# Token-major blocks turned by DMA instead of TensorE, and the two halves of the down product summed as one group

## The chip, the cores and the metric

The kernel runs on one core of a Trainium2 chip. The metric is the time of one execution on the device in microseconds (us). The engines are PE (TensorE; PEld is its weight load), DVE (VectorE), ACT (ScalarE), POOL (GpSimd) and SP (SyncE, whose queue issues nearly all DMAs here).

## The reference

A decoder trunk of two layers on 512 tokens of width 1024. Each layer is a feed-forward half step, a mixing step of three kinds of attention, and a second feed-forward half step:

```
def _swiglu(t, w_gate, w_up, w_down):
    return (jax.nn.silu(t @ w_gate) * (t @ w_up)) @ w_down

mem_n = _rmsnorm(mem, mem_norm_g)
for l in range(DEPTH):                      # 2
    f = _swiglu(_rmsnorm(h, ffn1_pre_g[l]), ffn1_w_gate[l], ffn1_w_up[l], ffn1_w_down[l])
    h = h + 0.5 * _rmsnorm(f, ffn1_post_g[l])
    ...                                     # mixing; uses mem_n @ w_mem_kv[l]
    f = _swiglu(_rmsnorm(h, ffn2_pre_g[l]), ffn2_w_gate[l], ffn2_w_up[l], ffn2_w_down[l])
    h = h + 0.5 * _rmsnorm(f, ffn2_post_g[l])
```

D_FF is 2816, which is 22 tiles of 128. Everything is float32.

## The kernel before

A float32 product is made of three matmuls (`mm3`, lines 204 to 206): each operand is split into a high and a low part, h = copy on ACT (L181), l = x - h on DVE (L182).

There are four feed-forward blocks, named a0, c0, a1, c1. In each, 16 of the 22 hidden tiles are computed in two halves (ci = 0, 1) of eight tiles, by a block scheme with seven products in place of eight: `token_products` makes the gate products G and the up products U, `products` the down products d. Tokens and columns are cut in two, a product multiplies sums of blocks, and `ORDER`, `SUM` and `TO` say in which order the seven run, into which pair of PSUM banks each adds up, and which block of the result is finished by it. One product is 24 matmuls of 128x512. The other six hidden tiles (16 to 21) are plain products: `halved`, `gates` and `ups`, called g and u in the plan, and their part of the down product is `down`, which also adds everything up and starts the normalisation of the next step.

G and U come out token-major: a block has tokens on the partitions. The down products need the hidden axis on the partitions. So after U's products n = 1, 4, 5 and 6 the finished block (gate times up, 128 x 1024 words, two token tiles by four hidden tiles) is turned by `turn` (L790): eight TensorE transposes into two PSUM banks (L800) and two copies to SBUF on ACT (L802). They are traced in the middle of the next product. `hidden_rows` holds the turned blocks.

`product` (L844) runs a down product. `first_factor` (L824) builds its left operand one product ahead. For the first half the results are copied to the f tiles (L874, L877) and added (L875, L879); the second half runs the same seven products again into other banks and adds its results to f on DVE; its n = 1 starts from a copy of f back into PSUM (L855).

The order of the work is a queue `Q` of jobs. A job has weight units and a generator of PE work. Before a job runs, its units are loaded, and the units of the jobs behind it, four units ahead (`load_ahead`): a load is a DMA on SP (`fetch`), for most block units a subtraction (L326), and the split. Buffers come from rings by tag: "wh" and "wl" have four buffers, a product uses two of each; raw weights use two "raw" and, within a block, two to four "o" buffers; first factors use "v" (six); the scratch tag of `tmp` has five; PSUM has four banks "z" and four "mm". `PLAN` is the list of jobs of a feed-forward block. In it a plain product (one of two tiles of a pair) follows every two down products:

```
PLAN = 7 * [("G", 0)] + [("m", 0)] + 7 * [("U", 0)] + 7 * [("G", 1)] + 6 * [("U", 1)] + [("a", 0), ("U", 1)]
downs = iter(6 * [("d", 0)] + [("a", 1), ("d", 0)] + 7 * [("d", 1)])
```

Instructions are put in order on each engine at build time by a scheduler that works with modelled durations; `keep_in_program_order` pins an instruction behind the one traced before it on the same engine. Each engine then runs its list strictly in order.

In the a blocks the memory input is normalised as well: `mem_norm` loads two tiles, scales them (L1034), transposes them on TensorE (L1041) and writes the split result (L1046, L1047). It is a job of its own (`aside`) ahead of `down`; its users are the memory keys (pmk) and values.

Of the kernel before, what the change touches and what calls it, by code (L numbers as in the profile page):

```python
# [9 lines left out]
F32 = mybir.dt.float32  # L10
F32R = mybir.dt.float32r
BF16 = mybir.dt.bfloat16
AF = mybir.ActivationFunctionType
# [9 lines left out]
def kernel(  # L23
# [578 lines left out]
    def ffn(l, src, wg, wu, wd, dst, name, spare, parked, plan, aside=None):  # L602
# [7 lines left out]
        hr = {}  # L610
# [128 lines left out]
        def token_product(ci, up, n, uns):  # L739
# [13 lines left out]
            for un in uns:  # L753
                for k in range(un.nk):
# [6 lines left out]
                    if kk == ND // 2 - 2:  # L761
                        yield from turn("z")
# [24 lines left out]
            if up and n in (1, 4, 5, 6):  # L787
                st["turn"] = (f"{nm}", g, r)

        def turn(tag):  # L790

            nm, g, r = st.pop("turn", (None, None, None))
            if nm is None:
                return
            g = g.rearrange("p f q -> p (f q)")
            for b in range(2):
                pt = pbank(tag, f"ht{nm}_{b}")
                for f in range(2):
                    for e in range(2):
                        nc.tensor.transpose(pt[:, (2 * f + e) * P:(2 * f + e + 1) * P],  # L800
                                            g[:, e * S + (2 * b + f) * P:][:, :P], ident[:])
                nc.scalar.copy(r[:, 2 * b:2 * b + 2], pt[:].rearrange("p (f q) -> p f q", f=2))  # L802
                yield 0.4
# [40 lines left out]
        def product(ci, n, uns):  # L844
            if n == 0 and ci == 0:
                RINGS["o"] = 2
                dst.begin()
            if n < 6:
                first_factor(ci, n + 1)
            if n in (0, 1, 2):  # L850
                st["b", SUM[n]] = [pbank("z", f"pd{name}_{ci}_{n}_{e}") for e in range(2)]
            pts = st["b", SUM[n]]
            if n == 1 and ci:
                for e in range(2):
                    nc.scalar.copy(pts[e][:], dst.fs[e][:, HF[0]])  # L855
            h, l = st["a", ci, n]
            opens, ends = n in (0, 2) or (n == 1 and not ci), n in (1, 4, 6)
            for un in uns:
                for k in range(un.nk):
# [6 lines left out]
                    if kk == FC // 2 - 2:  # L866
                        yield from turn("mm")
            if n == 0:
                return
            i, hf = TO[n]  # L870
            for e in range(2):
                f = dst.fs[2 * i + e][:, HF[hf]]
                if n == 1:
                    nc.scalar.copy(f, st["b", 0][e][:])  # L874
                    nc.vector.tensor_tensor(f, f, pts[e][:], ALU.add)  # L875
                elif ci == 0 and n in (2, 3, 6):
                    nc.scalar.copy(f, pts[e][:])  # L877
                else:
                    nc.vector.tensor_tensor(f, f, pts[e][:], ALU.add)  # L879

        def products(ci):

            keep = Keep(lambda k0: stile([P, 2, S], "o", f"bt{name}_{ci}_{k0}", F32)[:])
            w = wd[l, ci * FC * P:(ci + 1) * FC * P]
            for n in range(7):
                uns = [BlockUnit(n, w, FC // 2, k, 2, S, keep, f"d{name}_{ci}_{n}_{k}", ("raw", "o")[k // 2])
                       for k in range(0, FC // 2, 2)]
                if n == 4:
                    for un, of in zip(uns, had):
                        un.inherits(of)  # L890
                had = uns
                yield uns, (lambda n=n, uns=uns: product(ci, n, uns))
# [18 lines left out]
        def queue(what):  # L911
# [13 lines left out]
            else:  # L925
                if what not in made:
                    made[what] = products(n) if kind == "d" else token_products(n, kind == "U")
# [11 lines left out]
        if aside is not None:  # L939
            Q.add([], aside)  # L940
        hact = lambda k, c=FULL: (hid[f0 + k][:, 0, c], hid[f0 + k][:, 1, c])
        down(wd[l, f0 * P:], NF - f0, hact, f"d{name}", dst, marks, back, down_from)
        return marks

    def down(w, ktiles, act, name, dst, marks, before, begun=None):
# [52 lines left out]
        Q.add(uns[0], first)  # L998
        marks["next"] = [], []
# [697 lines left out]
```

## Time and profile before

| what | value |
|---|---|
| median of 3 runs | 2390.12 us (2388.59 to 2391.15) |
| profiled execution | 2389.31 us |
| its span, first to last instruction | 2387.6 us |
| mean granted TensorE clock | 0.998 |
| DMA | 338.23 MB, q1 busy 44.3% of 16 engines' span |

The page gives the busy time of each engine, its share of the span and the number of its instructions. A table by stretch gives, for each stretch from:to in us, its length, then for each engine the busy time and in brackets the count of instructions, then the granted clock, the share of the DMA engines and GB/s. A row of a timeline has start, duration, engine, line, operation, written tile <- read tiles, shape and count. A group row has line, engine, operation, tiles, shapes and count, then busy us and mean ns, then the engine's idle time before them with what ended it. In rows by line the three numbers behind a count are the shortest, median and longest duration in ns. A wait row has the waiting engine, tile and line, whom it waited for, us in total, times, and the longest.

### The profile page before, as it was taken

Reading aid. Unit: us, or ns where it says so; the run is one execution under the profiler, and the core shown is the slowest. Engines: PE = TensorE matmul, PEld = TensorE weight load, DVE = VectorE, ACT = ScalarE, POOL = GpSimd, SP = SyncE. Lnnn points to the kernel's source line nnn. Section 1 sums busy time; section 2 is a strip of 40 time slices with the busy share of each in tenths; the row PEclk is TensorE's granted clock in tenths of the full one; section 3 lists DMA queues with packets and bytes.
Section 4 is the critical chain, followed back from the end, with each engine's and each line's share of the span. In section 5 each row is a group of like instructions: output and inputs, shape, how many; then the busy total and the mean of one; then the engine's idle time right before and its main releaser. Section 6 shows DMA issues by size and latency. Waiting matters only on the chain.

```text
span 2387.6 us, 31555 instructions
## 1 busy us (share of the span) xinstructions
PE 2370.0 (99%) x11975; PEld 2006.6 (84%) x11975; DVE 1844.2 (77%) x2414; ACT 1425.1 (60%) x2250; POOL 75.1 (3%) x134
## 2 busy tenths in 40 slices
PE   9999999999999999999999999999999999999998
PEld 7888889888888888888888888888888888888887
DVE  8878877577777688788788788766777767887885
ACT  6655555576766555555655554656777664655554
POOL 1000000000111000000000000000001100000000
PEclk9999999999999999999999999999999999999999
DMA  6554455223323655444645554542323235555444
GB/s 205 184 150 158 142 189 147 80 82 87 89 72 106 195 175 175 144 158 157 206 140 167 150 176 156 187 116 71 98 71 97 80 115 198 164 176 154 154 140 153
DMA packets 232173, 338.23 MB, mean 142 GB/s; under 512 B 10683, under 2 KB 125395, under 8 KB 232021
## 3 DMA queue, kind: packets, MB, share of 16 engines
q1 hardware_dynamic: 231924, 336.18, 44.3%
q8 instruction: 94, 1.54, 0.3%
q14 instruction: 59, 0.48, 0.1%
q0 software_dynamic: 96, 0.03, 0.0%
HBM read 319.39 MB, written 16.78 MB: 141 GB/s over the span
## 4 chain that ended last, share of the span: by engine, by line
PE 89%; DVE 5%; DMA 3%; ACT 2%; issue 1%; SPq 0%; POOL 0%; DVEq 0%; ACTq 0%
PE pg L205 3%; PE pg L204 3%; PE pg L206 3%; PE pda L205 3%; PE pda L206 3%; PE pda L204 3%; PE pdc L205 3%; PE pdc L206 2%; PE pdc L204 2%; PE pb L206 1%; PE pb L205 1%; PE pb L204 1%; PE pq L205 1%; PE pq L204 1%; PE pq L206 1%
## 5 line engine op out<-in xcount | busy, mean ns | idle before, releaser
L204 PE MATMUL pg<-us_a,wh_wg 128*128 128x512 f32 x384 | 150.9, 393 | 0.0
L205 PE MATMUL pg<-us_a,wh_wg 128*128 128x512 f32 x384 | 149.8, 390 | 0.0
L206 PE MATMUL pg<-us_a,wl_wg 128*128 128x512 f32 x384 | 149.7, 390 | 0.0
L205 PE MATMUL pda<-wl_da,aha 128*128 128x512 f32 x224 | 87.6, 391 | 0.6 <-DVE wl_da L182 0.5
L205 PE MATMUL pdc<-wl_dc,ahc 128*128 128x512 f32 x224 | 87.5, 391 | 0.3 <-DVE wl_dc L182 0.3
L204 PE MATMUL pda<-wh_da,aha 128*128 128x512 f32 x224 | 87.4, 390 | 0.0
L204 PE MATMUL pdc<-wh_dc,ahc 128*128 128x512 f32 x224 | 87.4, 390 | 0.0
L206 PE MATMUL pda<-wh_da,ala 128*128 128x512 f32 x224 | 87.2, 389 | 0.0
L206 PE MATMUL pdc<-wh_dc,alc 128*128 128x512 f32 x224 | 87.2, 389 | 0.0
L206 PEld LDWEIGHTS pg<-us_a,wl_wg 128*128 128x128 f32 x384 | 72.1, 188 | 15.2
L204 PEld LDWEIGHTS pg<-us_a,wh_wg 128*128 128x128 f32 x384 | 72.1, 188 | 14.1
L205 PEld LDWEIGHTS pg<-us_a,wh_wg 128*128 128x128 f32 x384 | 72.2, 188 | 14.1
L182 DVE TENSOR_TENSOR wl_dc<-raw_dc,wh_dc 128x1024 fp32r<-128x1024 f32 x50 | 61.1, 1223 | 29.3 <-ACT wh_dc L181 29.1
L181 ACT CAST wh_dc<-raw_dc 128x1024 fp32r<-128x1024 f32 x50 | 52.6, 1053 | 43.9 <-PE pdc L206 15.1
L182 DVE TENSOR_TENSOR wl_da<-raw_da,wh_da 128x1024 fp32r<-128x1024 f32 x50 | 61.1, 1223 | 22.3 <-ACT wh_da L181 22.0
L181 ACT CAST wh_da<-raw_da 128x1024 fp32r<-128x1024 f32 x50 | 52.7, 1055 | 39.3 <-PE pda L206 15.0
L185 DVE SCALAR_TENSOR_TENSOR wl_wg<-raw_wg,wh_wg 128x1024 fp32r<-128x1024 f32 x48 | 58.4, 1220 | 21.6 <-ACT wh_wg L184 21.6
L199 DVE SCALAR_TENSOR_TENSOR ga<-pg,bgate,ga 128x512 f32<-128x512 f32 x48 | 35.9, 747 | 49.5 <-ACT ga L198 49.5
L181 ACT CAST wh_uc<-raw_uc 128x1024 fp32r<-128x1024 f32 x44 | 46.3, 1053 | 43.5 <-PE pwc1u L206 10.3
L181 ACT CAST wh_ua<-raw_ua 128x1024 fp32r<-128x1024 f32 x44 | 46.2, 1053 | 34.3 <-PE pwa1u L206 10.3
L184 ACT ACTIVATE wh_wg<-raw_wg 128x1024 fp32r<-128x1024 f32 x48 | 50.5, 1057 | 24.0 <-PE pv L1088 11.7
L182 DVE TENSOR_TENSOR wl_uc<-raw_uc,wh_uc 128x1024 fp32r<-128x1024 f32 x44 | 53.7, 1220 | 14.3 <-ACT wh_uc L181 14.2
(655 smaller groups left out, 8044.4 us busy)
## 6 DMA issues: line engine op xcount, KB each, us to landing
raw_da<-in_ffn_w_down_dram SPq DMA_DIRECT2D x66, 512.0 KB, 4.6
raw_dc<-in_ffn_w_down_dram SPq DMA_DIRECT2D x66, 512.0 KB, 5.3
raw_ga<-in_ffn_w_gate_dram SPq DMA_DIRECT2D x52, 512.0 KB, 3.9
raw_ua<-in_ffn_w_up_dram SPq DMA_DIRECT2D x52, 512.0 KB, 3.9
raw_gc<-in_ffn_w_gate_dram SPq DMA_DIRECT2D x52, 512.0 KB, 3.8
raw_uc<-in_ffn_w_up_dram SPq DMA_DIRECT2D x52, 512.0 KB, 3.8
raw_wg<-in_w_gate_dram SPq DMA_DIRECT2D x48, 512.0 KB, 3.5
raw_wo<-in_w_out_dram SPq DMA_DIRECT2D x24, 512.0 KB, 3.6
```

The costliest lines, as they stand in the source:

```text
L181: both = [nc.scalar.copy(h_ap, src)]
L182: make = lambda: nc.vector.tensor_tensor(l_ap, src, h_ap.bitcast(F32), ALU.subtract)
L184: both = [nc.scalar.activation(h_ap, src, AF.Copy, scale=scale)]
L185: make = lambda: nc.vector.scalar_tensor_tensor(l_ap, src, scale, h_ap.bitcast(F32), ALU.mult, ALU.subtract)
L199: nc.vector.scalar_tensor_tensor(t, z, minus, t, ALU.max, ALU.add)
L204: nc.tensor.matmul(pt, lh, rh, start=start, stop=False, skip_group_check=free)
L205: nc.tensor.matmul(pt, lh, rl, start=False, stop=False, skip_group_check=free)
L206: nc.tensor.matmul(pt, ll, rh, start=False, stop=stop, skip_group_check=free)
```

## The change

Three edits.

First, `turn` no longer uses TensorE. The block is looked at as two-byte words. Two ACT copies part the first and second halves of all words into two planes; one transposing DMA on SP turns each plane as eight 128x128 tiles; two ACT copies join the turned planes in `hidden_rows`. The steps have fixed places: the parting copies at the second step (kk = 1) of the next block product, the DMAs at its fourth (kk = 3), the joining copies at the first and second step of the block product two later; copies and DMAs are pinned in program order. Plain products between them are not counted. The planes lie in scratch tiles and, for n = 1 and 5, the turned ones in "rs".

Second, the down products of both halves run as one group, `DOWN`: n = 0 of both halves, n = 1 of both, and so on (n = 3 and 4 of one half together). Both halves add up in the same PSUM banks, so results are copied or added to f once. The bank pair of n = 1 is started by a copy of n = 0's. The plain products are spread among the 14 by the list 2, 2, 1, 1, 2, 2, 1, 1; n = 6 of both halves comes last.

Third, the job `mem_norm` stands behind the first job of `down` instead of ahead of it.

```diff
@@ token_product, product
-                    if kk == ND // 2 - 2:
-                        yield from turn("z")
+                    turn(kk)
...
             if up and n in (1, 4, 5, 6):
-                st["turn"] = (f"{nm}", g, r)
-
-        def turn(tag):
-
-            nm, g, r = st.pop("turn", (None, None, None))
-            if nm is None:
-                return
-            g = g.rearrange("p f q -> p (f q)")
-            for b in range(2):
-                pt = pbank(tag, f"ht{nm}_{b}")
-                for f in range(2):
-                    for e in range(2):
-                        nc.tensor.transpose(pt[:, (2 * f + e) * P:(2 * f + e + 1) * P],
-                                            g[:, e * S + (2 * b + f) * P:][:, :P], ident[:])
-                nc.scalar.copy(r[:, 2 * b:2 * b + 2], pt[:].rearrange("p (f q) -> p f q", f=2))
-                yield 0.4
+                turns.append([nm, g, (2 * ci + q[1], q[0]), n in (1, 5), 0, None])
+
+        def turn(kk):
+
+            later = tc.keep_in_program_order
+            for one in turns:
+                nm, g, (row, i), own, age, planes = one
+                if kk == 1 and age == 0:
+                    one[5] = planes = [tmp(f"th{nm}_{h}")[:].bitcast(U16) for h in range(2)]
+                    words = g.rearrange("p f q -> p (f q)").bitcast(U16)
+                    for h, plane in enumerate(planes):
+                        later(nc.scalar.copy(plane, words[:, h::2]))
+                if kk == 3 and age == 0:
+                    one[5] = ([stile([P, 2, 2 * S], "rs", "tr" + nm, U16)[:, h] for h in range(2)] if own else
+                              [tmp(f"tr{nm}_{h}")[:].bitcast(U16) for h in range(2)])
+                    for plane, part in zip(one[5], planes):
+                        later(nc.sync.dma_start_transpose(plane.rearrange("p (r q) -> p r q", q=P), part))
+                if kk in (0, 1) and age == 2:
+                    r = hidden_rows(row)[:].bitcast(U16)
+                    later(nc.scalar.copy(r[:, :, i * S + kk:(i + 1) * S:2].rearrange("p f (e q) -> p e f q", e=2),
+                                         planes[kk].rearrange("p (e f q) -> p e f q", e=2, q=P)))
+                if kk == ND // 2 - 1:
+                    one[4] += 1
+            turns[:] = [one for one in turns if one[4] < 3]
...
-        def product(ci, n, uns):
-            if n == 0 and ci == 0:
+        DOWN = [(ci, n) for ns in ((0,), (1,), (2,), (3, 4), (5,), (6,)) for ci in range(NC) for n in ns]
+
+        def product(at, uns):
+            ci, n = DOWN[at]
+            first, last = ci == 0, ci == NC - 1
...
-            if n < 6:
-                first_factor(ci, n + 1)
-            if n in (0, 1, 2):
-                st["b", SUM[n]] = [pbank("z", f"pd{name}_{ci}_{n}_{e}") for e in range(2)]
+            if at + 1 < len(DOWN):
+                first_factor(*DOWN[at + 1])
+            if first and n in (0, 2):
+                st["b", SUM[n]] = [pbank("z", f"pd{name}_{n}_{e}") for e in range(2)]
             pts = st["b", SUM[n]]
-            if n == 1 and ci:
-                for e in range(2):
-                    nc.scalar.copy(pts[e][:], dst.fs[e][:, HF[0]])
...
+            if not last:
+                return
             if n == 0:
+                st["b", 1] = [pbank("z", f"pd{name}_1_{e}") for e in range(2)]
+                for e in range(2):
+                    nc.scalar.copy(st["b", 1][e][:], pts[e][:])
                 return
             i, hf = TO[n]
             for e in range(2):
                 f = dst.fs[2 * i + e][:, HF[hf]]
-                if n == 1:
-                    nc.scalar.copy(f, st["b", 0][e][:])
+                if n in (4, 5):
                     nc.vector.tensor_tensor(f, f, pts[e][:], ALU.add)
-                elif ci == 0 and n in (2, 3, 6):
+                else:
                     nc.scalar.copy(f, pts[e][:])
-                else:
-                    nc.vector.tensor_tensor(f, f, pts[e][:], ALU.add)
...
-        if aside is not None:
-            Q.add([], aside)
...
@@ down
         Q.add(uns[0], first)
+        if aside is not None:
+            Q.add([], aside)
...
-    downs = iter(6 * [("d", 0)] + [("a", 1), ("d", 0)] + 7 * [("d", 1)])
-    for f in (18, 20):
-        for kind in "gu":
-            for m in range(2):
-                PLAN += list(itertools.islice(downs, 2)) + [(kind, f, m)]
+    downs = iter(14 * [("d", 0)])
+    slots = iter([(kind, f, m) for f in (18, 20) for kind in "gu" for m in range(2)])
+    for n in (2, 2, 1, 1, 2, 2, 1, 1):
+        PLAN += list(itertools.islice(downs, n)) + [next(slots)]
     PLAN += list(downs)
```

34 lines of the change are left out of this document (18 added, 16 removed).

## The prediction

> **What bounds the kernel now.** I read the head of the page first, then PE's own waits, then the stretches of the first feed-forward block, and last the timeline around one transposition.
>
> ```profile
> span 2387.6 us, 31555 instructions
> PE 2370.0 (99%) x11975; PEld 2006.6 (84%) x11975; DVE 1844.2 (77%) x2414; ACT 1425.1 (60%) x2250; POOL 75.1 (3%) x134
> ```
>
> PE is busy for all but 17.6 us, so only PE work taken away, or PE made to wait, can move the end. In two tables by stretch (us, then PE, PEld, DVE, ACT, POOL) the first has start, the four feed-forward blocks with their plain pairs, and end, and the second, for the first block, the U products (72 to 116 and 154 to 199), the second G products (116 to 154) and the down products (199 to 325):
>
> ```profile
> 0.00:14.00 14.00, 10.51 (x38) 5.49 (x39) 6.63 (x17) 8.77 (x16) 1.89 (x8) 0.88 0.85 280
> 14.00:320.00 306.00, 303.72 (x1459) 253.85 (x1459) 257.45 (x272) 178.38 (x222) 5.14 (x6) 1.00 0.52 166
> 855.00:1165.00 310.00, 309.37 (x1490) 259.09 (x1490) 256.01 (x255) 169.76 (x212) 0.00 (x0) 1.00 0.51 165
> 1196.00:1505.00 309.00, 308.29 (x1484) 257.98 (x1483) 255.57 (x258) 168.58 (x211) 0.00 (x0) 1.00 0.50 160
> 2040.00:2345.00 305.00, 304.11 (x1466) 254.65 (x1465) 254.36 (x253) 167.69 (x210) 0.00 (x0) 1.00 0.50 159
> 2345.00:2388.00 43.00, 35.33 (x156) 28.91 (x155) 22.76 (x37) 18.80 (x38) 0.00 (x0) 0.95 0.36 135
> ...
> 72.00:116.00 44.00, 43.67 (x201) 36.04 (x200) 37.91 (x46) 30.44 (x39) 0.00 (x0) 1.00 0.57 175
> 116.00:154.00 38.00, 38.00 (x177) 31.38 (x176) 28.68 (x28) 22.97 (x29) 0.00 (x0) 1.00 0.53 154
> 154.00:199.00 45.00, 44.82 (x210) 36.76 (x208) 35.42 (x34) 26.03 (x32) 0.00 (x0) 1.00 0.33 105
> 199.00:325.00 126.00, 125.48 (x566) 103.42 (x565) 103.69 (x102) 65.26 (x80) 0.00 (x0) 1.00 0.54 181
> ```
>
> Start and end hold 3.5 and 7.7 us of PE's idle time; the four blocks lose 2.3, 0.6, 0.7 and 0.9. PE's longest single wait in them is
>
> ```profile
> PE pwa0g L206 <- DVE ula L182: 1.1, 1, 1.1
> ```
>
> so tidier ordering is worth 4.5 us at the very most. DVE is at 79 to 86% in U, ACT at 58 to 69%: ACT has room for 14 to 19 us in each U stretch, DVE for 6 to 10. What the change adds to ACT must fit into that.
>
> **Transposes leave PE.** The timeline shows one transposition (eight of L800 as one row) among the matmuls:
>
> ```profile
> 94.67 0.39 PE L204 MATMUL pwa0u<-wh_ua,uha 128*128 128x512 f32 x1
> ...
> 97.84 0.39 PE L206 MATMUL pwa0u<-wh_ua,ula 128*128 128x512 f32 x1
> 98.07 1.03 PE L800 MATMUL hta0u<-ident,sa 128*128 128x128 f32 x8
> 98.86 0.48 PE L204 MATMUL pwa0u<-wh_ua,uha 128*128 128x512 f32 x1
> 99.18 0.40 PE L205 MATMUL pwa0u<-wl_ua,uha 128*128 128x512 f32 x1
> ```
>
> Matmuls overlap, so their price is the distance of starts: fourteen steps from 94.67 to 97.84 make 0.226 us each, and a product of 24 matmuls 5.44 us. The eight transposes hold PE from 98.07 to 98.86, 0.79 us, and the matmul behind them starts its successor after 0.32 instead of 0.23 us: 0.88 us in all. There are four such turns in each half of each block, 32 in the program (256 transposes, next row): 32 x 0.88 = **28.2 us** leave PE. Nothing else in the change alters the number of matmuls.
>
> ```profile
> 0.00:2388.00 2388.00, 33.15 (x256) 29.58 (x256) 1.00 0.45 142
> 0.00:2388.00 2388.00, 34.41 (x64) 1.00 0.45 142
> ```
>
> (The first is L800 alone, its busy time counting overlap; the second L802 alone on ACT.)
>
> **Copies on ACT.** The 64 copies of L802 (34.4 us in union) go. Each turn now has two copies that part the halves of the words and two that join them, each of 1024 two-byte elements in a partition: 128 in all. No such copy is in the trace. The nearest row is ACT's cast of 128x1024; half of it (half the bytes) is the lower end, twice it, 2.1 us (ACT passing over both halves of each word to take one), the upper.
>
> ```profile
> L181 ACT CAST wh_ua<-raw_ua 128x1024 fp32r<-128x1024 f32 x44 | 46.2, 1053 | 34.3 <-PE pwa1u L206 10.3 <-PE pwa0u L206 7.5 <-issue 4.1
> L182 DVE TENSOR_TENSOR wl_ua<-raw_ua,wh_ua 128x1024 fp32r<-128x1024 f32 x44 | 53.6, 1220 | 10.3 <-ACT wh_ua L181 10.2
> 187.00:209.00 22.00, 21.82 (x107) 17.70 (x107) 16.61 (x17) 12.72 (x17) 0.00 (x0) 1.00 0.36 117
> ```
>
> I take 1.05 us, since the element count is the same: 134 us come, 34 go, ACT carries 100 us more (33 to 234 at the two ends), 25 in each block. That is off PE's path as long as the weight splits (L181 on ACT, then L182 on DVE, 1.05 + 1.22 us) stay ahead. There are four buffers of each weight part, two in a product, so a split waits for the product two before its own ("<-PE pwa0u L206" above). It has one and a half products, 8.2 us, and needs 2.3: some 5.8 us of delay reach nobody. The densest place is the end of U with the start of the down products, the last row above: ACT works 12.7 us there, 9.5 without its three pairs of L802. In the four products n=5, n=6, down 0 and down 1 (21.8 us) twelve of the new copies fall, 12.6 us: 22.1 us of work, a backlog of 0.3. U's first half, running into the next G products, is as dense. Nothing is lost there.
>
> Two places have less slack. While a plain product holds its weights through two down products, only two buffers turn over, and a split has half a product less 2.3 us, that is 0.4. The last turn's joining copies (2.1 us) fall at the start of such a pair: 1.7 us once in each block at the worst, 7 in all. And n=1 opens on a bank that ACT copies for it (L746):
>
> ```profile
> 164.83 1.06 ACT L746 COPY pwa0u<-pwa0u 128x512 f32<-128x512 f32 x2
> 169.11 0.39 PE L204 MATMUL pwa0u<-wh_ua,us_x 128*128 128x512 f32 x1
> ```
>
> The copies end 3.2 us ahead of n=1's first matmul, so a joining pair in front of them stays hidden. I put this part at 3 us (ends 0 and 7).
>
> **Transposing DMAs.** Each turn issues two on SP's queue, 256 KB each. Issue is 0.37 us for a plain load; SP's time beyond that is unknown and lies between 0.37 and a few us. SP runs in order: while it waits for a parting copy or works on a transposing DMA, the weight fetches behind it wait, and the block subtractions and splits for them; a fetch may lose some 3 us so, and in U six raw buffers (two and four) run ahead by more than a product. The trace has no transposing DMA; landing is bounded by the shortest of that size and by the longest of any weight load (the last row, minimum/median/maximum):
>
> ```profile
> L296 SPq DMA_DIRECT2D raw_ua<-in_ffn_w_up_dram x40: 367/368/368, 56.4 to 1351.5; - x40
> gsave<-ga SPq DMA_DIRECT2D x16, 256.0 KB, 2.1
> gb<-gsave SPq DMA_DIRECT2D x16, 256.0 KB, 4.0
> DMA to landing us min/median/max: 3.3/4.3/10.8
> ```
>
> How long may it take? The parting copies stand behind ACT's previously issued split, which waits for the end of product p; they end 1.05 + 2.1 = 3.2 us after it. Two issues take 0.7. The joining copies stand behind the split that waits for the end of p+2, so ACT reaches them 2 x 5.44 + 1.05 = 11.9 us after the end of p. That leaves 8 us before ACT waits and, with 5.8 us of slack, some 14 before PE does. I take 4 us of landing, nearest to the 256 KB rows, and so nothing; at 10.8 ACT waits 2.8 us, hidden. The bytes, 64 x 256 KB = 17 MB on top of 338, are read and written on engines that are 33 to 57% busy in these stretches.
>
> The Trainium skill speaks against this: VectorE: DVE Perf Modes, "The three transpose paths" and "Rules for kernel authors", gives 1309 ns for a 128x128 two-byte block by DMA against 390 ns on TensorE and advises TensorE where PSUM will do. Taken block after block, sixteen blocks would be an estimated 21 us in a turn, too late, and the sum would be that of the slower rival below. Advanced Engine Details and Errata, "X-Bar Transpose (TRN2)", says instead that transposing DMAs are as fast as plain ones; by that the sum stays as it is. No row here decides between the two.
>
> **The down group.** The two halves now add up in the same PSUM banks.
>
> ```profile
> L875 DVE TENSOR_TENSOR fa<-fa,pda x8: 678/680/687, 211.1 to 1459.8; 128x512 f32<-128x512 f32 x8
> L879 DVE TENSOR_TENSOR fa<-fa,pda x28: 675/680/689, 239.3 to 1500.3; 128x512 f32<-128x512 f32 x28
> L855 ACT COPY pda<-fa x4: 577/579/580, 262.3 to 1447.4; 128x512 f32<-128x512 f32 x4
> ```
>
> With the same counts again for c blocks, DVE loses 16 + 56 adds and keeps 16: 56 x 0.68 = 38 us, 9.5 in each block. ACT does 40 copies instead of 48, 5 us less. None of it is on PE's path now. The new waits (b0 copied into b1 before n=1, b1 emptied before n=2 takes its banks, b0 emptied before n=5 and before n=6) are two copies or adds, 1.2 to 1.4 us, and each has a plain product or another down product, 5.44 us, in front of PE's next use; without that cover each would cost 1.3 us, 5 us in a block. Four block tiles in place of two share the eight "o" buffers with two fetched ones and the hidden units: the third and fourth hidden unit may wait for n=6's loads; they are used only in the last down product, two products later, so nothing. This order can win back part of the 4.5 us of small waits; I take 0.5.
>
> **Memory's normalisation.** Its 16 transposes stay. It moves behind the first plain down tiles, 36 matmuls or 8.2 us later, and its two loads behind the reload of h on SP. Its user, pmk, starts at 356.9; its own PE work starts at 321.7:
>
> ```profile
> L204 PEld LDWEIGHTS pmk<-mn,wh_mk x64: 187/192/192, 356.9 to 1552.5; 128*128 128x128 f32 x64
> L1041 PE MATMUL mt<-ident,mraw x32: 270/272/328, 321.7 to 1507.0; 128*128 128x128 f32 x32
> ```
>
> The 35 us between cover 8.2. If loads came late by more than that, SP's order would be at fault; priced at nothing.
>
> **Sum.** -28.2 - 0.5 + 3 = -25.7 us against the profiled execution (2389.31 us, 0.8 below the median of 2390.12). On the median: **2364 us**. The bounds of the terms move it from 2390.1 - 28.2 - 4.5 = 2357 to 2390.1 - 28.2 + 7 = 2369; with a few us for DMAs that crowd the weight loads, 2373.
>
> **Rivals.**
> - *ACT becomes the second bound (2373 to 2410).* At 1.6 us a copy the dense four products carry 19.2 + 9.5 us in 21.8: a backlog of 6.9, 1.1 past the slack, in two places of each block; the held pair loses 3.2 - 0.4 = 2.8. 4 x (2 x 1.1 + 2.8) = 20 us come back: 2382. At about 1.7 the whole gain is gone, at 2.1 it is slower by some 40. For it: strided two-byte elements are new here, and DVE already waits for ACT in the L182 row. Against: DVE gets lighter in the down stretch, and ACT's rows go by elements.
> - *Transposes land too late (slower).* ACT, in order, waits at the joining copy and the weight splits behind it come late. It decides from a landing of about 14 us; by 15.2 the 28 us are eaten. Of the four turns in a half, one starts its DMA a product after another and shares its delay; three wait in full, 24 in all. If a pair goes one after the other, each at the longest landing seen, 10.8 us, that is 21.6 us: 24 x (21.6 - 14) = 182 us, less 28: 2544 us. For it: two-byte elements, and nothing in this trace excludes it. Against: loads of 512 KB land in 4.3 us at the median. The skill's first page above, with its 21 us, gives this rival's size.
> - *No change (2385 to 2395).* The waits just eat 28 us. Nothing speaks for just this size.
>
> **How the numbers follow.** Forecast 0.58; ACT bound 0.21 (0.15 faster, 0.03 within 0.2%, 0.03 slower); late transposes 0.18; no change 0.03. A measurement here can tell 0.2%, 4.8 us. Faster: 0.58 + 0.15 = 0.73; same 0.06; slower 0.21. The range takes the forecast and the ACT rival up to no change, 2357 to 2390 us, 0.78, and leaves out what is slower.
>
> **What would show it.** L800 and L802 gone; PE's busy time near 2342 us; 128 copies of two-byte elements near 1.05 us; transposing DMAs landing under 8 us; 16 adds in place of the 72 of L875 and L879; PE's idle time in a block still 1 to 3 us. Wrong would be: PE waiting for wl tiles in U or at the first down products, with ACT waiting for a DMA before them (late transposes), or with ACT at 90% there and no DMA wait (ACT bound), or SP busy for microseconds in one transposing issue with weight loads landing late behind it.

## The result, and the profile after

The changed kernel takes **2410.22 us** (median; 2409.67 to 2411.48) beside 2389.72 for the kernel before: a ratio of 1.0084, 95% interval 1.0072 to 1.0097. The prediction, 2364 us (2357 to 2390), is wrong, and on the wrong side: 20.5 us slower instead of 25.7 faster.

The head of the page after. Its lines have moved: the operand splits are L182 and L183, the matmuls L205 to L207, the bank copy of n = 1 is L747, the parting copies are L799, the transposing DMAs L804, the joining copies L807.

```profile
span 2408.2 us, 31180 instructions
PE 2358.9 (98%) x11719; PEld 1986.5 (82%) x11719; DVE 1804.7 (75%) x2358; ACT 1515.6 (63%) x2306; POOL 75.5 (3%) x134
```

PE does 256 instructions less, but its busy time falls by 11 us only, where 28 were forecast, and its idle time grows from 17.6 to 49.3 us. PE's waits say where:

```profile
PE pwc1g L205 <- ACT pwc1g L747: 7.3, 1, 7.3
PE pwa1g L205 <- ACT pwa1g L747: 6.9, 1, 6.9
PE pwc0g L205 <- ACT pwc0g L747: 6.8, 1, 6.8
PE pwa0g L205 <- ACT pwa0g L747: 6.6, 1, 6.6
PE pdc L206 <- DVE wl_dc L183: 1.8, 4, 0.5
```

One long wait in each of the four blocks, always at the same place: the first matmul of n = 1 in the second half's G products waits for the bank that ACT copies for it. 27.6 us in all. PE's timeline at the first of them:

```profile
128.99 0.39 PE L207 MATMUL pwa0g<-wh_ga,ula 128*128 128x512 f32 x1
135.97 0.80 PE L205 MATMUL pwa0g<-wh_ga,us_x 128*128 128x512 f32 x1 [6.58 <-ACT pwa0g L747]
136.56 0.63 PE L206 MATMUL pwa0g<-wl_ga,us_x 128*128 128x512 f32 x1
136.99 0.63 PE L207 MATMUL pwa0g<-wh_ga,us_x 128*128 128x512 f32 x1
...
140.40 0.43 PE L206 MATMUL pwa0g<-wl_ga,us_x 128*128 128x512 f32 x1
140.67 0.39 PE L207 MATMUL pwa0g<-wh_ga,us_x 128*128 128x512 f32 x1
```

The wait costs twice. Behind it the matmuls start 0.427 us apart instead of 0.227 (nine steps from 136.56 to 140.40), and the eleven steps from 135.97 to 140.67 take 4.70 us in place of 2.49: 2.2 us more. In the table by stretch the granted clock of this one falls to 0.92:

```profile
116.00:160.00 44.00, 37.42 (x157) 30.43 (x156) 27.75 (x27) 33.88 (x36) 0.00 (x0) 0.92 0.68 171
```

The Trainium skill, TensorE: Matmul & The Clock Gate, "What's actually happening", says that the array's clock is halved after an idle window of some 3.4 us and comes back after a busy one. The trace agrees: 0.427 is nearly twice 0.227, and the slow stretch lasts 4.4 us. The prediction had no such term. So each of the four places costs about 6.9 + 2.2 = 9 us, 36 in all (the slow stretches of the other three cost 1.7, 3.0 and 2.4 us).

Why is the copy late? ACT's timeline before it, first in the kernel before (the row of 126.57 is the bank copy, and the last row is n = 1's first matmul on PE), then in the changed one:

```profile
115.67 1.05 ACT L181 CAST wh_ga<-tga 128x1024 fp32r<-128x1024 f32 x1 [2.28 <-PE pwa0u L206]
...
122.03 1.05 ACT L181 CAST wh_ga<-raw_ga 128x1024 fp32r<-128x1024 f32 x1 [1.67 <-PE pwa0g L206]
...
126.57 1.06 ACT L746 COPY pwa0g<-pwa0g 128x512 f32<-128x512 f32 x2
...
130.87 0.39 PE L204 MATMUL pwa0g<-wh_ga,us_x 128*128 128x512 f32 x1
```

```profile
112.49 1.34 ACT L807 COPY hra<-tra0u 128x1024 uint16<-128x1024 uint16 x1
116.27 1.05 ACT L182 CAST wh_ga<-tga 128x1024 fp32r<-128x1024 f32 x1 [2.44 <-PE pwa0u L207]
118.50 1.36 ACT L807 COPY hra<-tra0u 128x1024 uint16<-128x1024 uint16 x1 [1.17 <-DMA tra0u<-tha0u]
119.72 1.99 ACT L799 COPY tha0u<-sa 128x1024 uint16<-128x1024 uint16 x2
121.61 1.05 ACT L182 CAST wh_ga<-tga 128x1024 fp32r<-128x1024 f32 x1
122.56 1.04 ACT L799 COPY tha0u<-sa 128x1024 uint16<-128x1024 uint16 x1
124.10 1.05 ACT L799 COPY tha0u<-sa 128x1024 uint16<-128x1024 uint16 x1 [0.49 <-DMA tra0u<-tha0u]
125.05 2.00 ACT L182 CAST wh_ga<-raw_ga 128x1024 fp32r<-128x1024 f32 x2
126.96 2.57 ACT L807 COPY hra<-tra0u 128x1024 uint16<-128x1024 uint16 x2
129.39 1.98 ACT L799 COPY tha0u<-sa 128x1024 uint16<-128x1024 uint16 x2
131.28 1.99 ACT L182 CAST wh_ga<-tga 128x1024 fp32r<-128x1024 f32 x2
133.17 1.33 ACT L807 COPY hra<-tra0u 128x1024 uint16<-128x1024 uint16 x1
134.37 1.05 ACT L775 COPY sa<-pwa0g 128x512 f32<-128x512 f32 x2
135.31 1.08 ACT L747 COPY pwa0g<-pwa0g 128x512 f32<-128x512 f32 x2
136.30 3.86 ACT L807 COPY hra<-tra0u 128x1024 uint16<-128x1024 uint16 x3
```

From 112.49 to the bank copy ACT now has six parting and five joining copies (L799 and L807, by their counts), and from 118.50 on it never pauses but for 0.49 us. The bank copy starts 8.7 us later than before. It had 3.2 us to spare (127.6 to 130.87).

The rest of the page is near the forecast. Parting copies, joining copies and the DMAs' issue, for the block a0, and the DMAs' landing:

```profile
L799 ACT COPY tha0u<-sa x16: 1032/1042/1049, 101.6 to 216.0; 128x1024 uint16<-128x1024 uint16 x16
L807 ACT COPY hra<-tra0u x16: 1327/1358/1378, 112.5 to 225.5; 128x1024 uint16<-128x1024 uint16 x16
L804 SPq DMA_TRANSPOSE tra0u<-tha0u x16: 1231/1239/1443, 107.2 to 220.3; - x16
DMA to landing us min/median/max: 3.0/3.2/5.7
```

In the down group one add and one copy are left, with the same counts for c blocks, and memory's transposes start 14 us later, at the cost of one wait of 0.4 us for their input:

```profile
L887 DVE TENSOR_TENSOR fa<-fa,pda x8: 679/680/682, 288.9 to 1505.9; 128x512 f32<-128x512 f32 x8
L889 ACT COPY fa<-pda x16: 578/588/590, 235.0 to 1521.0; 128x512 f32<-128x512 f32 x16
L1052 PE MATMUL mt<-ident,mraw x32: 270/272/329, 335.9 to 1535.6; 128*128 128x128 f32 x32
```

### The profile page after: what moved, and what is told of

Its sections match the earlier page's. It is cut to its first block, busy times and chain, and to the rows that moved or that the text cites. A ratio compares the mean times of both kernels' runs of the same rounds, so it can differ in the third digit from the quotient of the medians.

```text
span 2408.2 us, 31180 instructions
## 1 busy us (share of the span) xinstructions
PE 2358.9 (98%) x11719; PEld 1986.5 (82%) x11719; DVE 1804.7 (75%) x2358; ACT 1515.6 (63%) x2306; POOL 75.5 (3%) x134
## 4 chain that ended last, share of the span: by engine, by line
PE 83%; ACT 6%; DMA 5%; DVE 4%; issue 2%; SPq 0%; DVEq 0%; ACTq 0%
PE pg L206 3%; PE pg L205 3%; PE pg L207 3%; PE pdc L206 3%; PE pdc L207 3%; PE pdc L205 3%; PE pda L206 2%; PE pda L207 2%; PE pda L205 2%; PE pq L206 1%; PE pq L205 1%; PE pk L206 1%; PE pq L207 1%; PE pk L207 1%; PE pk L205 1%
## 5 line engine op out<-in xcount | busy, mean ns | idle before, releaser
L205 PE MATMUL pg<-us_a,wh_wg 128*128 128x512 f32 x384 | 150.9, 393 | 0.0
L207 PE MATMUL pg<-us_a,wl_wg 128*128 128x512 f32 x384 | 149.7, 390 | 0.0
L183 DVE TENSOR_TENSOR wl_da<-raw_da,wh_da 128x1024 fp32r<-128x1024 f32 x50 | 60.8, 1223 | 47.8 <-ACT wh_da L182 47.5
L183 DVE TENSOR_TENSOR wl_dc<-raw_dc,wh_dc 128x1024 fp32r<-128x1024 f32 x50 | 61.0, 1223 | 44.5 <-ACT wh_dc L182 44.2
L205 PE MATMUL pda<-wh_da,aha 128*128 128x512 f32 x224 | 86.5, 390 | 1.3 <-ACT wh_da L182 1.3
L205 PE MATMUL pdc<-wh_dc,ahc 128*128 128x512 f32 x224 | 86.6, 391 | 1.0 <-ACT wh_dc L182 1.0
L207 PE MATMUL pdc<-wh_dc,alc 128*128 128x512 f32 x224 | 86.9, 389 | 0.0
L207 PE MATMUL pda<-wh_da,ala 128*128 128x512 f32 x224 | 86.9, 389 | 0.0
L207 PEld LDWEIGHTS pg<-us_a,wl_wg 128*128 128x128 f32 x384 | 72.1, 188 | 15.1
L205 PEld LDWEIGHTS pg<-us_a,wh_wg 128*128 128x128 f32 x384 | 72.1, 188 | 14.2
L182 ACT CAST wh_da<-raw_da 128x1024 fp32r<-128x1024 f32 x50 | 52.3, 1052 | 48.1 <-DMA raw_da<-in_ffn_w_down_dram 13.2
L182 ACT CAST wh_dc<-raw_dc 128x1024 fp32r<-128x1024 f32 x50 | 52.3, 1049 | 44.2 <-DMA raw_dc<-in_ffn_w_down_dram 12.0
L182 ACT CAST wh_uc<-raw_uc 128x1024 fp32r<-128x1024 f32 x44 | 46.4, 1053 | 40.1 <-PE pwc0u L207 10.3
L182 ACT CAST wh_ua<-raw_ua 128x1024 fp32r<-128x1024 f32 x44 | 46.2, 1052 | 33.1 <-PE pwa1u L207 10.3
L183 DVE TENSOR_TENSOR wl_ga<-raw_ga,wh_ga 128x1024 fp32r<-128x1024 f32 x40 | 48.3, 1221 | 22.4 <-ACT wh_ga L182 22.2
```

Source lines behind the costliest of these rows:

```text
L182: both = [nc.scalar.copy(h_ap, src)]
L183: make = lambda: nc.vector.tensor_tensor(l_ap, src, h_ap.bitcast(F32), ALU.subtract)
L205: nc.tensor.matmul(pt, lh, rh, start=start, stop=False, skip_group_check=free)
L207: nc.tensor.matmul(pt, ll, rh, start=False, stop=stop, skip_group_check=free)
```

## The experiments

Three readings stood at the start (theories 1, 2 and 3 in the expectations): that only the place of the n = 1 bank copies is at fault; that the transposing DMAs are (SP's queue, or ACT waiting for them); that ACT has too much to do, wherever it is put. Theory 4 is that the down group costs. Each ratio is to the kernel before, timed beside the run (2388.7 to 2390.0 us).

### The parts of the change, one by one

**e1_bank_early**: the bank copies of n = 1 are traced at the end of n = 0.

```
-            if n == 1:
-                for e in range(2):
-                    nc.scalar.copy(st["c", 1][e][:], st["c", 0][e][:])
...
             if n == 0:
+                st["c", 1] = [pbank("mm", f"pw{nm}_1_{e}") for e in range(2)]
+                for e in range(2):
+                    nc.scalar.copy(st["c", 1][e][:], st["c", 0][e][:])
                 return
```

> The changed kernel with one edit: ACT's two copies that open n=1's bank pair in G and U are traced when n=0's matmuls are done, a product earlier. Theory 1 (ACT's queue: in each block's second G half the bank copy stands behind the new parting and joining copies, PE waits 6.6 to 7.3 us, and then runs 11 matmuls at 0.43 instead of 0.23 us each): these four waits go, 4 x (6.9 + 2.4) = 37 us, 2373 us, ratio to before about 0.993. Theory 2 (transposing DMAs are late and hold ACT): the wait moves to the weight splits behind, 2400 us or more. Theory 3 (ACT simply has too much to do there, any order): PE waits as long for wh or wl tiles in the second G half, 2395 to 2410.

Measured: 2407.25 us, ratio 1.0075 (1.006 to 1.009). The four waits fall to 2.0 to 3.1 us, 10.8 in place of 27.6, and hardly anything is won: others grow (wl for a0's U products 2.4 us, wl for the output projection 2.7, wl for a0's G 2.0), so PE's idle time is still 40.7 us for 49.3, and its busy time grows by 3.9. Moving the one late copy alone makes other work late. The time lies in the ranges of the second and the third reading; e4 and e6 below decide against either as the whole cause.

**e2_turn_only** (the kernel before with `turn` changed, nothing else) and **e3_group_only** (the down group and memory's normalisation changed, the turn still on PE):

> The kernel before with the transposition by DMA alone; down products, plan and memory's normalisation as before. Theory 1: the four waits of about 7 us in the second G half stay, since they lie ahead of the down products; 2410 to 2416 us. If the down group is what costs (theory 4), this is near 2375 to 2385.

> The kernel before with the down group, its plan and memory's normalisation a job later; blocks transposed on TensorE as before. Theory 1: nothing of the loss is here, 2386 to 2391 us. Theory 4 (the group costs): 2400 or more.

Measured: the turn alone 2416.60 us, ratio 1.0116 (1.0099 to 1.0133), with waits of 6.5 to 7.9 us at the four places and, in the down products of each kind of block, 4.9 us of waits for wh; the group alone 2390.42, ratio 1.0003 (0.9994 to 1.0013). The loss is the turn's. Group and normalisation are worth nothing alone, as forecast, but take 6.4 us off the turn's cost.

**e4_no_dma**: the two `dma_start_transpose` go, the joining copies read the parted planes (the blocks stay unturned).

> The changed kernel without its 64 transposing DMAs: the joining copies read the parted planes, so the turned blocks are left unturned. All ACT copies stay. Theory 1: ACT's work and order are the same, the waits shrink only by ACT's 2 to 3 us of DMA waits in each block, perhaps 4.5 us left of 7 at n=1: 2395 to 2402 us. Theory 2: the waits go, 2375 us.

Measured: 2397.95 us, ratio 1.0038 (1.0023 to 1.0053). The four waits stay at 5.8 us each. So the copies by themselves bring the kernel above its old time, and the DMAs beside them cost 12 us more.

### Less on ACT, or later on ACT

**e5_pool_part** gives the parting copies to POOL, **e7_pool_both** the joining copies as well (`nc.scalar.copy` becomes `nc.gpsimd.tensor_copy`). **e6_spread** joins n = 4, 5 and 6 one block product later (`age == 3` instead of 2; n = 1 stays at 2; the age of a turn is 0 in the block product behind the one that finished its block). **e8_spread_bank** is e6 with the early bank copies of e1.

> The changed kernel with the 64 parting copies on POOL, which is idle for 97% of the span, instead of ACT; joining copies stay on ACT. Theory 3 (ACT has too much to do between the end of U's first half and the third product of the second G half: fourteen copies of 1.04 and 1.36 us in some 22 us): six to eight of those fourteen leave ACT, the waits of 6.6 to 7.3 us at n=1 fall under 2 us, and the time comes to 2370 to 2380 us, faster than before. Rival (the order on ACT alone, or the transposing DMAs): waits stay above 4 us, 2395 or more. Rival (POOL's reads hold up DVE, whose subtractions have two SBUF inputs): DVE's 1.22 us subtractions lengthen beside the copies and PE waits for wl tiles, 2390 or more.

> The changed kernel with the joining copies of the turns of n = 4, 5 and 6 one block product later, so that no product has parting and joining copies of two turns but one. The work of ACT is the same in all. Theory 3 in its local form (only the crowding matters): the wait at n=1 of the second G half stays, as n=4's joining pair now stands just ahead of the bank copy, but two joining pairs fewer lie ahead of it: 2 to 4 us of the 7 are left, 2390 to 2400 us. If nothing but total load counted: 2407 to 2413.

> The changed kernel with all 128 parting and joining copies on POOL. Theory 3: ACT has 34 us less to do than in the kernel before, no PE wait of the new kind is left, and PE's 28 us are won: 2360 to 2368 us. If POOL takes much longer for a joining copy than ACT's 1.36 us (two-byte writes four bytes apart), the turned blocks come late and PE or DVE waits for them: 2370 to 2400. If POOL holds up DVE: above 2380.

> The joining copies one product later and the bank copies of n=1 a product earlier. Theory 3, local form: the bank copy has only parting copies and n=4's earlier work ahead of it, its wait goes, and the splits have room: 2376 to 2388 us, a gain over before. Total load: PE waits for wh and wl tiles as in the run with the early bank copy alone, 2400 to 2407.

| run | us | ratio (95%) | the four waits at n = 1 |
|---|---|---|---|
| e5_pool_part | 2394.36 | 1.0018 (1.0009 to 1.0028) | 0.4 or less |
| e6_spread | 2386.55 | 0.9983 (0.9973 to 0.9992) | 0.9 to 1.6 |
| e7_pool_both | 2453.98 | 1.0269 (1.0253 to 1.0284) | none above 1 |
| e8_spread_bank | 2394.96 | 1.0021 (1.0012 to 1.0031) | moved: 1.4 to 3.3 for L775; up to 1.1 left |

L775 copies a result out of PSUM (called a drain below). The main forecasts of e5, e7 and e8 missed by 14, 86 and 7 us.

POOL takes the waits at n = 1 away and makes others. PE's waits in e7, and a row of the copies by line in e5 and in e7:

```profile
PE pda L206 <- DVE wl_da L183: 15.4, 8, 4.0
PE pdc L206 <- DVE wl_dc L183: 13.6, 8, 3.2
```

```profile
L799 POOL COPY tha0u<-sa x16: 1037/1770/2047, 97.1 to 203.4; 128x1024 uint16<-128x1024 uint16 x16
```

```profile
L807 POOL COPY hra<-tra0u x16: 1332/2310/2343, 112.4 to 231.3; 128x1024 uint16<-128x1024 uint16 x16
```

Clear of DVE's work a copy on POOL is as fast as on ACT (in e7, 1.04 us for the parting and 1.34 to 1.35 for the joining one); beside DVE it takes up to 2.4 us, and DVE's subtractions, 1.22 us otherwise, take up to 2.32. Sorted by overlap in e7's trace, the 66 subtractions for low parts of weights that share over half of their time with such a copy take 1.91 us in the mean, the 452 clear of them 1.22. The Trainium skill, SBUF — State Buffer, "SBUF: two separate sides", says that a DVE operation with two SBUF inputs and a GpSimd operation that reads SBUF share a port pair, and that the later one waits for the other's whole instruction; the lengths in this trace agree. Late low parts of the weights are what PE then waits for. In e8 PE waits for the drains instead, so e6 alone is better.

e6 has the same 128 copies and ACT is as busy (1515.0 us for 1515.6), and 24 of the 46 us between forecast and result are back. For these 24 us the amount of work on ACT is not the cause; its place is.

### The floor, and the DMAs by themselves

**e9_no_turn**: `turn` does nothing, the products go straight into the down factor's rows and stay unturned. **e10_dma_only**: the DMAs stay, the copies go; nothing reads what the DMAs write.

> The changed kernel with no turn at all: no parting copies, no transposing DMAs, no joining copies; the products are multiplied straight into the down factor's rows and stay unturned (this leaves the transposition out). It measures the floor under the turn. If the 28.2 us that the transposes gave up on PE are real and everything that the change lost comes from the turn's own instructions, the time is 2389.6 - 28.2 = 2361 to 2364 us and the four waits at the n = 1 bank copy of 7 us are gone. If something else binds once PE is shorter (the weight fetches, the splits on DVE, the granted clock), it stays above 2375, and then part of the loss was never the turn's.

> The changed kernel with its 64 transposing DMAs at their places and none of the 128 copies: each DMA reads the gate's block and its result is read by nothing; the products go unturned into the down factor's rows (the transposition is left out). With the run without DMAs and the run without any turn it makes a square of four. If the two costs add, the DMAs cost by themselves what they cost beside the copies, 12 us (2410.2 - 2398.0): 2374 us. If they cost only because a joining copy on ACT stands waiting for their landing, nothing of it is left here: 2362 to 2365. If they cost by holding SP for 1.24 us each and so delaying weight fetches, PE's waits for wh and wl (weights raw -> split) stay as many as in the changed kernel.

Measured: 2358.02 us, ratio 0.9871 (0.9857 to 0.9884), and 2358.41, ratio 0.9875 (0.986 to 0.989). The engines' line of e9's page, and the landing of e10's DMAs:

```profile
PE 2342.6 (99%) x11719; PEld 1981.6 (84%) x11719; DVE 1804.8 (77%) x2358; ACT 1382.3 (59%) x2178; POOL 75.1 (3%) x134
```

```profile
DMA to landing us min/median/max: 3.1/4.2/5.6
```

This settles two things. The 28.2 us are real: without the turn the changed kernel is 30.7 us faster than the kernel before, and PE is busy for 2342.6 us, the forecast's 2342. And 64 transposing DMAs by themselves cost nothing that these runs can tell. e9's span of 2357.1 us is the floor under the runs with copies: the changed kernel stands 51.1 us above it, 34.8 of them PE's idle time (49.3 for 14.5) and 16.3 its slower matmuls (2358.9 for 2342.6); 36 of the 51 are the four places.

### Where the joining copies go

**e11_late_joins**: as e6, and in the first half n = 5 joins at age 5, n = 6 at age 6, in the second half's G products n = 4 and n = 6. **e12_late_all**: as e11, and n = 1 joins at age 3.

```
-                turns.append([nm, g, (2 * ci + q[1], q[0]), n in (1, 5), 0, None])
+                turns.append([nm, g, (2 * ci + q[1], q[0]), n in (1, 5), 0, None, {1: 2, 5: 3 if ci else 5, 6: 3 if ci else 6}.get(n, 3)])
...
-                nm, g, (row, i), own, age, planes = one
+                nm, g, (row, i), own, age, planes, join = one
...
-                if kk in (0, 1) and age == 2:
+                if kk in (0, 1) and age == join:
```

> As the spread kernel, and the first half's joins of n = 5 and n = 6 wait until the second half's G products n = 4 and n = 6 (ages 5 and 6 instead of 3), where ACT has idle time between its casts. By the theory that the loss is ACT's crowded queue around n = 1 of the second half's G products, the rest of the wait there (1.6, 1.3, 1.2 and 0.9 us and the slow matmuls behind them) goes: 2380 to 2383 us. By the theory that what is left of the loss sits at the start of the down products and in the DMAs, nothing moves: 2385.5 to 2387.5.

> As the run with late joins, and the joins of n = 1 one block product later too (age 3 instead of 2), in both halves. The second joining copy of n = 1 waited 1.0 us for its DMA with five copies queued behind it; a product later its block has landed. By ACT's queue as the cause: 1 to 3 us less than the run with late joins, 2378 to 2382. If the copy's wait only trades places with copies that crowd the next product: no change against that run, within 1 us.

Measured: e11 **2373.79 us, ratio 0.994 (0.9928 to 0.9952), faster than both kernels**; e12 2409.16, ratio 1.0089 (1.0076 to 1.0103). e12's expectation (2378 to 2382) missed by 27 us. ACT is busy for 1514.8 and 1516.4 us: the same work. e11's ACT around the bank copy, then e12's SP and ACT:

```profile
128.69 1.05 ACT L747 COPY pwa0g<-pwa0g 128x512 f32<-128x512 f32 x2
129.68 0.58 ACT L775 COPY sa<-pwa0g 128x512 f32<-128x512 f32 x1
...
131.11 2.57 ACT L807 COPY hra<-tra0u 128x1024 uint16<-128x1024 uint16 x2
```

```profile
106.56 1.34 SPq L804 DMA_TRANSPOSE tra0u<-tha0u  x1
107.96 4.29 SPq L297 DMA_DIRECT2D raw_ga<-in_ffn_w_gate_dram  x3
113.04 3.47 SPq L804 DMA_TRANSPOSE tra0u<-tha0u  x2
...
120.69 1.25 SPq L804 DMA_TRANSPOSE tra0u<-tha0u  x1
```

```profile
123.75 1.38 ACT L807 COPY hra<-tra0u 128x1024 uint16<-128x1024 uint16 x1 [2.14 <-DMA tra0u<-tha0u]
...
131.61 2.52 ACT L807 COPY hra<-tra0u 128x1024 uint16<-128x1024 uint16 x2
134.00 1.05 ACT L775 COPY sa<-pwa0g 128x512 f32<-128x512 f32 x2
134.95 1.06 ACT L747 COPY pwa0g<-pwa0g 128x512 f32<-128x512 f32 x2
```

In e11 the bank copies stand ahead of the drains and of n = 4's joins; in e12 they stand behind both and start 6.3 us later, and the four waits of 6.9 us are back. Ahead of that, n = 1's second joining copy waits 2.14 us for its DMA. That DMA is the one of 120.69, 14 us behind its twin at 106.56: the copy starts 3.06 us after this issue, and the two transposes between, of 113.04, have landed by 119.2. Three later runs take this apart.

**e13_first_half** delays the joins in the first half alone, **e14_late_dma2** and **e15_all_dma2** are e11 and e12 with the DMAs traced one k-step earlier (`kk == 2`).

> Later joins in the first half alone (n = 4 at age 3, n = 5 at 5, n = 6 at 6, n = 1 at 2); the second half, whose blocks the down product waits for, joins at age 2 as in the changed kernel. If the loss is the queue on ACT ahead of the n = 1 bank copies of the second half's G products, nearly all of the gain of the run with late joins is here: 2374 to 2380 us, and the four waits there are 1 us each. If the joins that run into the down product weigh as much, it keeps half of the loss: 2388 to 2395.

> As the run with late joins, and the transposing DMAs one k-step earlier in the program (behind kk = 2 instead of kk = 3, 1.36 us of PE). If a joining copy's wait for a plane whose DMA stood on SP behind weight fetches is what is left of the loss around that place (0.9 and 0.35 us of ACT there, 1.3 us later), it ends 1 to 4 us sooner than the late joins: 2370 to 2373. If SP, reaching the transposes sooner, now waits for the parting copies with the weight fetches behind it, it is slower: 2375 to 2385.

> As the run with every join later (2409 us), with the transposing DMAs one k-step earlier. If that run lost its gain because its second n = 1 joining copy waited 2.1 us for its DMA and everything behind it on ACT, the bank copies too, slid by 6 us, it comes back most of the way: 2374 to 2385. If it lost it because two more copies of 1.36 us now stand between the partings and the bank copies, whatever the DMA does, it stays at 2400 to 2412, with the waits of 7 us at n = 1.

Measured: e13 2382.36 us, ratio 0.9968 (0.9956 to 0.9981): of the 36 us that e11 wins over the changed kernel, 28 come from the first half's joins, the place ahead of the bank copies, and 9 from the second half's, which run into the down products. e14 2374.12, 0.9937 (0.9925 to 0.995), no different from e11; e15 2410.97, 1.0093 (1.0078 to 1.0109), no different from e12. The wait for the DMA is still there in e15 (2.15 us), so this run did not tell wait from order: in both runs SP issues the transposes at the same places among the weight fetches as without the edit.

**e16_late_no_dma** and **e17_all_no_dma** are e11 and e12 without DMAs, **e18_n4_behind** is e12 with n = 4's joins at age 4 in the first half, behind the bank copies.

> As the run with late joins (2374 us), without the 64 transposing DMAs: the joining copies read the parted planes, for n = 1 and 5 parted straight into the tile that held the turned ones (the blocks stay unturned, so this leaves part of the computation out). It is the control for the next run. The bank copies stand ahead of n = 4's joins as before; without DMA waits on ACT: 2362 to 2372 us.

> As the run with every join later (2409 us), without the transposing DMAs in the same way (the blocks stay unturned). The earlier transposes had left the wait of 2.1 us on ACT where it was; here it is gone for certain. If that wait made the difference of 35 us between the two runs, this one comes to within 5 us of its control without DMAs. If the order does it (n = 4's joins and the drains of n = 2 ahead of the n = 1 bank copies on ACT), it stays 20 us or more above its control, with waits of 5 us or more at the four bank copies.

> As the run with every join later (2409 us), DMAs and all, and the joins of n = 4 in the first half one block product later still (age 4, in n = 1 of the second half's G products, so traced behind its bank copies). If the order ahead of the bank copies is the cause, the four waits of 6.9 us go down to 2 us or less and the time to 2370 to 2382. If ACT is late for another reason (the DMA wait, the copies of n = 1), the waits stay above 4 us and the time above 2392.

Measured: e16 2369.37 us, ratio 0.9916 (0.9903 to 0.993); e17 2370.44, 0.992 (0.9907 to 0.9934); e18 2403.08, 1.006 (1.0046 to 1.0074), with four waits of 4.5 us. Without DMAs the difference of 35 us between the two placings is 1. With them, taking n = 4's pair from in front of the bank copies gives 2.4 us at each place, 6 us in all, and no more. So the reading that the pair of joins ahead of the bank copies makes the difference fell: it is a sixth of it. The rest comes with the transposing DMAs. How much of that is the 2.1 us wait for the late one is not shown: without DMAs the scheduler also lays the list otherwise (in e17 one of the two bank copies stands ahead of n = 4's joins), and the runs don't part the two. e11 itself stays 15.1 us above e9's span (2372.2 us), 8.6 of it in PE's idle time (23.1 for 14.5); what is left lies in waits of about 1 us at the four places and at the start of the down products, and wasn't followed further.

## Why the prediction was wrong

**Transposes leave PE, 28.2 us: right.** PE's busy time in e9 is the forecast to within a microsecond.

**Copies on ACT: size right, place wrong. This is the step that failed.** The parting copy was forecast at 1.05 us and takes 1.04; the joining copy takes 1.36, 30% more. That the total fits is luck: 64 of each are 154 us by their rows, but copies that follow each other overlap, and the 128 add 133 us to ACT's busy time (1515.6 in the changed kernel for 1382.3 in e9) where the sum had 134. The step that failed is "U's first half, running into the next G products, is as dense. Nothing is lost there", with the one on n = 1, "a joining pair in front of them stays hidden". Both looked at the wrong thing:
- The dense place was reckoned as work against time, 22.1 us in 21.8, and its slack as the 5.8 us of the weight splits. PE hardly waits for splits after the change. It waits for the bank copy, whose slack is 3.2 us, as forecast, and in front of which stand not one joining pair but eleven copies of four turns.
- ACT's idle time was taken as free. Between the same cast (108.7 before, 108.8 after) and the bank copy, ACT's rows hold 8.4 us of idle time before and 5.8 after, while its work grows by 11.3: 8.7 us later in all. Most of the pauses end when PE or a DMA lets go of a buffer (2.44 and 1.17 us in the rows above), and ACT, in order, can't use them for what stands further back.
- The slow matmuls behind each wait, about 2.2 us a place, were in no term of the sum.

**Held weight pair, 3 us (0 to 7) together with the n = 1 bank copies: too small.** Leaving out the four places above, PE waits 2.2 us for wh of the plain products there, 2.3 for wh and 3.2 for wl of the down products: 7.7 us, where the kernel before has 0.8.

**Transposing DMAs at nothing: right by themselves, wrong beside the copies.** Landing takes 3.2 us at the median where 4 were taken, and e10 costs 0.4 us. The step "Two issues take 0.7", from which it got "That leaves 8 us before ACT waits", failed as well. In SP's list the two issues of the first turn are 6.6 us apart, with three weight fetches between them:

```profile
107.25 1.35 SPq L804 DMA_TRANSPOSE tra0u<-tha0u  x1
108.65 4.29 SPq L297 DMA_DIRECT2D raw_ga<-in_ffn_w_gate_dram  x3
113.86 1.24 SPq L804 DMA_TRANSPOSE tra0u<-tha0u  x1
```

So ACT waits for the second (1.17 us at 118.50), just where it has no time. What the DMAs cost hangs on where the copies stand:

| copies | without DMAs | with DMAs | difference |
|---|---|---|---|
| none (e9, e10) | 2358.0 | 2358.4 | 0.4 |
| late joins (e16, e11) | 2369.4 | 2373.8 | 4.4 |
| as changed (e4, the changed kernel) | 2398.0 | 2410.2 | 12.3 |
| all joins later (e17, e12) | 2370.4 | 2409.2 | 38.7 |

The intervals are some 3 us wide to either side, so 0.4 is nothing and 4.4 hardly more.

Of the two pages weighed there, Advanced Engine Details and Errata, "X-Bar Transpose (TRN2)", of the Trainium skill agrees with the trace: 256 KB land in 3.2 us, between the 2.1 and 4.0 of the plain rows. The 1309 ns a block of the Trainium skill's VectorE: DVE Perf Modes, "The three transpose paths", taken block after block, would be an estimated 10.5 us for the eight blocks of one DMA; the measured 3.2 us decide against reading it so.

**The down group at 0.5 us and memory's normalisation at nothing: right by themselves.** DVE's busy time falls by 39.5 us (38 forecast), and e3 is 0.03% from the kernel before. Beside the turn the two are worth 6.4 us (e2), which the sum did not have.

**The rivals.** "ACT becomes the second bound" named the right engine for the wrong reason, and that 2410 stands at the end of its range is luck. Its price, 1.6 us a copy, didn't come, nor did its sign, ACT at 90%: from 112 to 140 us ACT is busy for 23.9 of 28 us, 85%, in the changed kernel and just as long in e11, where PE is busy for 27.3 us of the 28 instead of 20.7. "Late transposes" did not come as priced; a DMA that was late by its place in SP's list, not by its landing, did (e12).

## What to carry to other kernels

When work goes to an engine that has room, don't weigh it against the engine's idle time. Find the instruction on that engine that PE waits for with the least slack (here a copy of 1 us with 3.2 us to spare), and count what will stand in front of it in the engine's list, with the waits of those instructions as well. Then move the consumers of an asynchronous step away from that place, and look what the scheduler makes of it, transfers included, since later is not always better (e12): the same 128 copies and 64 DMAs made 2374 us or 2410.

## What the runs showed of the hardware that was not expected

- A strided two-byte copy on ACT costs by its elements, but not by them alone: 1.04 us where it takes every second word half and writes densely, 1.36 us where it reads densely and writes every second one (POOL clear of DVE: 1.04 and 1.34 to 1.35).
- SP is held 1.24 us by the issue of a transposing DMA, for 0.37 us by that of a plain load.
- Between POOL's copies and DVE's subtractions, both sides take up to nearly twice their time (2.32 for 1.22 us, 2.40 for 1.34).
- A gap of 6.6 to 7.3 us on PE costs 1.7 to 3.0 us more behind it, and one of 4.5 us (e18) costs no less: 1.8 to 2.6.
